# Transformer block on one core: the first two Strassen products take operands without the norm's factor, VectorE's order is written out through the first two chunks, and x is held in half tiles

## The chip, the cores and the metric

One core of one Trainium2 chip runs the kernel. The metric is the device time of one execution in microseconds (us); three executions of the kernel before took 1358.51 to 1360.71, median 1359.51.

## What is computed

The reference is one layer of a hybrid encoder, for one sequence of 1024 positions, model width 1024, all in float32. Cut to what matters here:

```python
x = x + jnp.concatenate([y_conv, y_mla], axis=-1) @ w_o[i]

hf = rmsnorm(x, norm_ffn_g[i])
a = dwconv_centred(hf @ w_up[i], ffn_conv_w[i], ffn_conv_b[i])
g, u = jnp.split(a, 2, axis=-1)
x = x + (jax.nn.silu(g) * u) @ w_down[i]

gate = jax.nn.sigmoid(rmsnorm(x, ple_norm_g[i]) @ w_ple_gate[i])
x = x + gate * (p[i] @ w_ple_proj[i])
```

`rmsnorm(x, g)` is x times g, times one factor r per position (the inverse root of the mean square). `w_up` has 2 x 2816 columns: 22 chunks of 128 columns of g and of u.

## The kernel before, in words

**Layout.** x lies with its 1024 features on partitions, in 8 blocks of 128, and the 1024 positions along the rows. A matrix product of float32 is made of three matmuls of parts: each operand is split into a high part (rounded, made by ScalarE) and a low part (what is left, made by VectorE), and high x high, high x low and low x high are summed in PSUM. `gemm` (L135) issues these. A sum of 128 x 512 fills one of the eight banks of PSUM.

**Stages around the change.** After attention, `out_mla` (L606) adds the second half of the output projection block by block (d = 0 to 7): VectorE adds the sum to x (L625), ScalarE squares it, VectorE adds the squares to `ss`, and SyncE's queue stores the block to DRAM for later (L627). Then the position factors r of the norm are made: `norm` (L217) sums `ss` over partitions by 16 little matmuls (L228), takes the inverse root on VectorE (L233 to L242), and spreads r over all partitions by 16 more little matmuls (L253) into two banks. The little matmuls are put between the matmuls of other work. That other work is `embed` (L774): the per-layer embedding's projection, eight blocks of twelve matmuls that need neither x nor the norm.

**The chunks.** Each chunk's up projection is a Strassen-Winograd product with 7 products in place of 8: the moving operands are sums and differences of the quarters of the normed x (`up_moving`, L716; b11, b21, b22, t1 to t4, each in four blocks k, shared by all chunks), the stationary ones are sums of the weights (`stationary`, L640: a11, a12, s1 to s4, a22). Quarters: x blocks 0 to 3 or 4 to 7, positions 0 to 511 or 512 to 1023. Each product is twelve matmuls of 128 x 512. `BANK` (L672) says which products add into the same bank: 1 and 2; 6, 7 and 4; 5 and 3. After each product `read` (L793) takes the bank's sum so far, and the next product into that bank has to wait for this. With both halves of g read, VectorE and ScalarE make the convolution over positions (`conv3`, L256) and ScalarE makes Silu (L815).

**Order.** TensorE's order is that of the code throughout. VectorE's is the code's inside a `manual_schedule` block (L821 to L850), outside of which a scheduler sets it by its own estimate; ScalarE's and GpSimd's are the scheduler's always. Before, the block ends when the moving operands are made, so that the reads, the convolutions and the weights of the chunks are placed by the scheduler. TensorE's order in the stage is: embeddings 0 to 5, product 1 of chunks 0 and 1, embeddings 6 and 7, and then products 5, 2, 3, 6, 7, 4, each of chunk 0 and then of chunk 1; chunk 2 and the rest follow in `run` (L694).

Of the kernel before, what the change touches and what calls it, by code (L numbers as in the profile page):

```python
# [33 lines left out]
def tile_block(ctx, tc, xT, pT, wlat, wun, wdn, wuq, wukv, vecs, cst, out):  # L34
# [180 lines left out]


    def norm(sh, sl, dim):  # L217
        n = sh.shape[1] // P
# [4 lines left out]

        def first():
            p8.append(small())
            for t in range(n):
                for i, z in enumerate((sh, sl)):
                    tiny.append(lambda t=t, i=i, z=z: mm(p8[0][:, 2 * t:2 * t + 2], z[:, t * P:t * P + P], onesr[:, 0:2], start=i == 0, stop=i == 1))  # L228

        def root():  # L230
            v, y, t = [const.tile([P, 8], F32, name=m, bufs=2)[:, 0:n] for m in ("nv", "ny", "nt")]
            yh, yl = [const.tile([P, 8], FR, name=m, bufs=2)[:, 0:n] for m in ("nyh", "nyl")]
            ts(out=v, in0=p8[0][:, 0:2 * n:2], scalar1=1.0 / dim, scalar2=EPS, op0=ALU.mult, op1=ALU.add)  # L233
            yi = y.bitcast(I32)
            ts(out=yi, in0=v.bitcast(I32), scalar1=1, scalar2=None, op0=ALU.logical_shift_right)
            ts(out=yi, in0=yi, scalar1=-1.0, scalar2=float(0x5F3759DF), op0=ALU.mult, op1=ALU.add)
            for _ in range(3):
# [2 lines left out]
                stt(out=y, in0=t, scalar=1.5, in1=y, op0=ALU.add, op1=ALU.mult)  # L240
# [1 line left out]
            vt(out=yl, in0=y, in1=f(yh), op=ALU.subtract)  # L242
# [4 lines left out]
        def second():
            for t in range(n):
                if t % 4 == 0:
                    rs.append(small()[:, 0:min(4, n - t) * P])  # L250
                c = t % 4 * P
                for i, y in enumerate(ys):
                    tiny.append(lambda p=rs[-1][:, c:c + P], y=y[:, t:t + 1], i=i: mm(p, y.to_broadcast([P, P]), identr, start=i == 0, stop=i == 1))  # L253
# [367 lines left out]
    for d in range(NC_):  # L621
        out_mla(d, [3] if d < 3 else [0, 1, 2, 3])
        if d < 7:
            for p, s in pieces(accs[d]):
                tt(out=x1[d][:, s], in0=p, in1=x1[d][:, s], op=ALU.add)  # L625
            square_acc(ss, x1[d], d == 0, nc.vector)
        nc.sync.dma_start(out=x2d[d], in_=x1[d]) if d < 7 else None  # L627
# [86 lines left out]
    def up_moving(rs, then):  # L716
# [4 lines left out]
        def scaled(c, i):
            o = x1[c][:, HALF[i]]
            stt(out=o, in0=o, scalar=vc(V_FFN + c), in1=rs[i], op0=ALU.mult, op1=ALU.mult)

        def diff(o, p, q):
            tt(out=o, in0=p, in1=q, op=sub)  # L726

        def behind(fn):
            if low[0]:
                low[0]()  # L730
            low[0] = fn

        def put(src, h, z):
            nc.scalar.copy(out=h, in_=src)
# [50 lines left out]
    def up_unit(c, later=None):  # L785
# [6 lines left out]

        def read(i, p):  # L793
            g1, g2, u1, u2 = ag[:, T1S], ag[:, T2S], au[:, T1S], au[:, T2S]
            if i == 1:
                nc.scalar.copy(out=u1, in_=p)
# [15 lines left out]
            if i in (3, 6) and len(half) == 2:  # L812
# [2 lines left out]
                act(out=t, in_=t, func=AF.Silu)  # L815
# [6 lines left out]
    sq, sh, sl = ft(), ft(FR), xt.tile([P, S], FR, name="xt")  # L822
    for p, s in pieces(accs[7]):
        tt(out=x1[7][:, s], in0=p, in1=x1[7][:, s], op=ALU.add)
        act(out=sq[:, s], in_=x1[7][:, s], func=AF.Square)
    for s in HALF:
# [3 lines left out]
    nc.sync.dma_start(out=x2d[7], in_=x1[7])  # L830
# [9 lines left out]
    for d in range(6):  # L840
        if d == 2:
            norm_first()
        if d == 4:
            norm_second()
# [1 line left out]
        if d == 2:
            norm_root()
        if d == 4:
            up_moving(rs, lambda: pair.append(up_unit(1, weights1)))
# [1 line left out]
    weights1.pop()()
    for i in (1, 5, 2, 3, 6, 7, 4):
        for unit in pair:
            unit.step(i)
        if i == 1:
            embed(6)
            embed(7)
    for c in range(2, NFF):
# [267 lines left out]
```

## Time and profile before

The profiled execution is one of the same program. Busy time is the time in which an engine has an instruction in it.

| | |
|---|---|
| median of three executions | 1359.51 us |
| the profiled execution | 1359.67 us |
| its span, first to last instruction | 1357.7 us |
| TensorE (PE) busy | 1325.2 us, 98% |
| VectorE (DVE) busy | 1006.2 us, 74% |
| ScalarE (ACT) busy | 597.0 us, 44% |
| GpSimd (POOL) busy | 256.5 us, 19% |
| mean granted clock of TensorE | 0.989 |

In the lists of instructions a row has: start and duration in us from the start of the span, engine, line of the kernel, operation, tiles out<-in, shape, count, and in brackets how long the engine had been idle before and what ended that. Names are those of the tiles: `xt` holds x, `b` the moving operands, `wm` and `whi`/`wlo` the weights, `bk` a PSUM bank, `tmp` working tiles. PEclk is the clock granted to TensorE as a share of full speed.

### The profile page before, as it was taken

To read this page: it belongs to the slowest core of one execution; us is meant where nothing else is said; L and a number is where in the kernel's file an instruction comes from. 1 tells how busy PE (TensorE), PEld (TensorE's weight loads), DVE (VectorE), ACT (ScalarE), POOL (GpSimd) and SP (SyncE) were. 2 spreads that over 40 slices of the span, in tenths; PEclk is the share of its full clock that TensorE was granted. 3 is DMA by queue.
4 is the path that set the end of the run, shared out by engine and by line. 5 is a ranking of instruction groups with operands and counts; after the bars stand their busy time and mean duration, and the time that the engine had idled before them with its cause. 6 is when DMAs were issued, how large, how long until landed. Compare 5 with 4: busy or idle time off the path is not lost.

```text
span 1357.7 us, 16448 instructions
## 1 busy us (share of the span) xinstructions
PE 1325.2 (98%) x6354; PEld 1089.3 (80%) x6354; DVE 1006.2 (74%) x1336; ACT 597.0 (44%) x839; POOL 256.5 (19%) x214
## 2 busy tenths in 40 slices
PE   9999999999999999879999999999998999999997
PEld 7877788888888887658888888888877888888897
DVE  7478923799999957988888888888665555557787
ACT  5323422688888834543443444344331111125433
POOL 0276452455545510000000000000000000000000
PEclk9999999999999999979999999999999999999998
DMA  6201134200000154203222222222165232121123
GB/s 210 83 31 47 47 125 155 78 1 17 1 17 1 64 215 171 93 16 124 78 78 78 94 78 78 78 93 74 66 233 216 96 98 94 55 78 51 52 81 113
DMA packets 38894, 117.38 MB, mean 86 GB/s; under 512 B 4256, under 2 KB 9632, under 8 KB 38816
## 3 DMA queue, kind: packets, MB, share of 16 engines
q1 hardware_dynamic: 36976, 111.49, 23.3%
q10 hardware_dynamic: 1840, 4.83, 0.9%
q8 instruction: 50, 0.82, 0.3%
q14 instruction: 28, 0.23, 0.1%
HBM read 88.00 MB, written 28.31 MB: 86 GB/s over the span
## 4 chain that ended last, share of the span: by engine, by line
PE 87%; DVE 9%; issue 2%; DMA 1%; ACT 1%; POOL 1%; POOLq 0%; SPq 0%; ACTq 0%
PE bk L139 55%; PE big L139 12%; PE small L139 4%; PE small L534 4%; PE small L547 2%; PE big L504 2%; PE big L508 2%; PE big L506 2%; PE small L546 2%; DVE tmp L163 1%; DVE xt L726 1%; DVE b L726 1%; DMA x<-x2d 1%; DVE tmp L262 1%; DVE rbc L164 0%
## 5 line engine op out<-in xcount | busy, mean ns | idle before, releaser
L139 PE MATMUL bk<-gu,whi 128*128 128x512 f32 x704 | 194.4, 397 | 4.1 <-DVE x L904 3.5
L139 PE MATMUL bk<-b,wm 128*128 128x512 f32 x792 | 192.8, 396 | 1.7 <-DVE b L726 1.4
L139 PEld LDWEIGHTS bk<-b,wm 128*128 128x128 f32 x792 | 148.5, 188 | 38.7 <-DVE b L726 2.5
L139 PEld LDWEIGHTS bk<-gu,whi 128*128 128x128 f32 x704 | 132.7, 189 | 37.1 <-issue 3.9
L904 DVE TENSOR_TENSOR x<-bk,x 128x512 f32<-128x512 f32 x112 | 72.0, 686 | 90.0 <-PE bk L139 87.3
L139 PE MATMUL bk<-xt,wm 128*128 128x512 f32 x528 | 129.4, 399 | 7.4 <-DVE xt L726 5.4
L128 ACT ACTIVATE whi<-wraw 128x1024 fp32r<-128x1024 f32 (+2 forms) x55 | 51.3, 933 | 193.0 <-PE bk L139 140.2
L139 PEld LDWEIGHTS bk<-xt,wm 128*128 128x128 f32 x528 | 100.9, 192 | 32.5 <-DVE xt L726 7.7
L139 PE MATMUL bk<-b,whi 128*128 128x512 f32 x352 | 112.3, 399 | 3.1 <-DVE b L726 3.1
L646 POOL TENSOR_TENSOR wm<-wraw,wm 128x512 fp32r<-128x512 f32 x22 | 28.8, 1309 | 449.2 <-ACT wm L645 449.2
L139 PE MATMUL bk<-gu,wlo 128*128 128x512 f32 x352 | 111.3, 397 | 0.0
L790 DVE TENSOR_TENSOR tmp<-bk,tmp 128x512 f32<-128x512 f32 x110 | 75.6, 688 | 30.7 <-PE bk L139 30.6
L521 POOL TENSOR_SCALAR tmp<-tmp,sm 128x256 f32<-128x256 f32 x64 | 70.1, 1095 | 101.4 <-DVE sm L514 98.8
L261 ACT ACTIVATE tmp<-tmp,vec 128x1024 f32<-128x1024 f32 x44 | 54.4, 1237 | 71.0 <-DVE tmp L790 71.0
L511 DVE TENSOR_REDUCE mx<-big 128x1 f32<-128x1024 f32 x64 | 78.0, 1219 | 10.3 <-PE big L508 9.8
L537 DVE TENSOR_TENSOR ptl<-small,pth 128x512 fp32r<-128x512 f32 x128 | 83.1, 680 | 1.2 <-ACT pth L536 0.9
L139 PEld LDWEIGHTS bk<-b,whi 128*128 128x128 f32 x352 | 66.9, 190 | 20.5 <-DVE b L726 4.4
L262 DVE SCALAR_TENSOR_TENSOR tmp<-tmp,vec 128x1023 f32<-128x1023 f32 x48 | 63.9, 1331 | 21.5 <-ACT tmp L261 19.0
L139 PEld LDWEIGHTS bk<-gu,wlo 128*128 128x128 f32 x352 | 66.4, 189 | 16.1
L536 ACT CAST pth<-small 128x512 fp32r<-128x512 f32 x128 | 68.9, 591 | 19.8 <-PE small L534 17.3
L971 POOL TENSOR_TENSOR tmp<-x,rf 128x256 f32<-128x256 f32 x3 | 2.1, 727 | 385.2 <-ACT rf L966 385.2
L139 PE MATMUL big<-hh,whi 128*128 128x512 f32 x224 | 71.8, 402 | 3.1 <-DVE tmp L414 3.1
(290 smaller groups left out, 2863.0 us busy)
## 6 DMA issues: line engine op xcount, KB each, us to landing
wraw<-in_wun_dram SPq DMA_DIRECT2D x73, 512.0 KB, 3.2
gud<-tmp SPq DMA_DIRECT2D x22, 512.0 KB, 2.6
tmp<-gud SPq DMA_DIRECT2D x22, 512.0 KB, 4.0
wraw<-in_wdn_dram SPq DMA_DIRECT2D x24, 384.0 KB, 3.1
tmp<-in_xT_dram SPq DMA_DIRECT2D x15, 512.0 KB, 4.2
x1d<-tmp SPq DMA_DIRECT2D x8, 512.0 KB, 2.8
xt<-x1d SPq DMA_DIRECT2D x8, 512.0 KB, 6.7
x2d<-xt SPq DMA_DIRECT2D x8, 512.0 KB, 2.7
```

Source lines behind the costliest of these rows:

```text
L128: act(out=wh, in_=raw, func=AF.Copy)
L139: mm(p, w, x[:, s], start=a, stop=z, skip_group_check=more)
L261: act(out=t, in_=src, func=AF.Identity, scale=vc(w + 1), bias=vc(bias))
L262: stt(out=t[:, 1:S], in0=src[:, 0:S - 1], scalar=vc(w), in1=t[:, 1:S], op0=ALU.mult, op1=ALU.add)
L511: nc.vector.tensor_reduce(m, p, AX.X, ALU.max, negate=True)
L521: nc.gpsimd.tensor_scalar(out=e[:, w:S], in0=e[:, w:S], scalar1=su, scalar2=None, op0=ALU.mult)
L534: nc.tensor.transpose(t[:, k, :], e[:, (g * 4 + k) * P:(g * 4 + k) * P + P], ident)
L536: nc.scalar.copy(out=pth[:, ks, qs], in_=t)
L537: tt(out=ptl[:, ks, qs], in0=t, in1=f(pth)[:, ks, qs], op=ALU.subtract)
L646: eng.tensor_tensor(out=z, in0=src, in1=f(h), op=ALU.subtract)
L790: add = lambda o, p, q: tt(out=o, in0=p, in1=q, op=ALU.add)
L904: tt(out=x1[d][:, s], in0=q, in1=x1[d][:, s], op=ALU.add)
```

## The change

It has four parts.

1. The moving operands b11 and b21 are split from x times the gain g alone (`raw_moving`), before r is known. r is put on the sums when they are read: VectorE multiplies the sums of products 1 and 1 + 2 by r in place of a copy by ScalarE. This holds for all 22 chunks. ScalarE copies r from the two banks to SBUF once (`rr`). The other moving operands are made of the normed x as before, one small function each (`put_t1`, `put_b22`, `put_t3`, `put_t2`, `put_t4`).
2. Product 1 and then product 2 of chunk 0 follow embedding 3, ahead of embeddings 4 to 7; product 1 and 2 of chunk 1 follow these; then 5, 5, 3, 3, 6, 6, 7, 7, 4, 4. The squares' little matmuls stand in embedding 1, those of r in embedding 3.
3. The block in which VectorE's order is the code's now reaches to the end of chunks 0 and 1, with the reads (`got`), both gate convolutions and chunk 2's weights in it.
4. x is held in 16 tiles of 128 x 512 instead of 8 of 128 x 1024, and loaded, added to, squared and stored by halves.

The core of the diff:

```diff
     for d in range(NC_):
-        nc.sync.dma_start(out=x1[d], in_=x1d[d])
+        for x, s in zip(x1[d], HALF):
+            nc.sync.dma_start(out=x, in_=x1d[d][:, s])
...
-        def step(self, i):
+        def step(self, i, read=True):
...
-            self.read(i, p)
+            if read:
+                self.got(i)
+
+        def got(self, i):
+            self.read(i, self.banks[BANK[i]])
...
+    def raw_moving(name, c0, tiles):
         for k in range(4):
+            x, g = x1[c0 + k][0], vc(V_FFN + c0 + k)
+            h, z = tiles(k)
+            act(out=h, in_=x, func=AF.Copy, scale=g)
+            behind(lambda x=x, g=g, h=h, z=z: stt(out=z, in0=x, scalar=g, in1=f(h), op0=ALU.mult, op1=ALU.subtract))
+            bs[k][name] = (h, z)
+        behind(None)
...
-            if i == 1:
-                nc.scalar.copy(out=u1, in_=p)
+            if i in (1, 2):
+                tt(out=u1 if i == 1 else g1, in0=p, in1=rr[:, T1S], op=ALU.mult)
             elif i == 5:
                 add(u2, p, u1)
-            elif i == 2:
-                nc.scalar.copy(out=g1, in_=p)
...
+    raw_moving("b11", 0, lambda k: (b1(), b1()))
+    embed(0)
+    embed(1, norm_first)
+    norm_root()
     for j in range(2):
         embed_weights(j)
...
+    raw_moving("b21", 4, lambda k: [z[:, T1S] for z in b2s[k]])
+    embed(2)
+    norm_second()
+    embed(3)
+    u0 = pair[0]
+    u0.step(1, False)
+    for i in range(2):
+        nc.scalar.copy(out=rr[:, HALF[i]], in_=rs[i])
+    put_t1(0, rs)
+    put_t1(1, rs)
+    u0.got(1)
+    u0.step(2, False)
...
+    for d in range(4, NC_):
         embed(d)
...
+    u0.step(6, False)
+    put_t4(1)
+    put_t4(2)
+    u0.got(6)
+    u1.step(6, False)
+    put_t4(3)
+    behind(None)
+    u1.got(6)
+    u2 = up_unit(2, weights1)
+    u0.step(7)
+    weights1.pop()()
+    u1.step(7)
+    u0.step(4)
+    u1.step(4)
     dve_order.close()
```

VectorE, ahead of `out_mla(6)` (`s14` and `s23` are sums of chunk 0's weights; `big_4753` and `big_4725` are the sum of block 4; `wlo_4834` and `wlo_4800` the low part of the weights that block 6 needs). Before:

```order
L625 TENSOR_TENSOR xt_4545<-big_4725,xt_4545 128x1024
L654 TENSOR_TENSOR s14_4873<-wraw_4867 128x512
L657 TENSOR_TENSOR s23_4874<-wraw_4865,wraw_4867 128x512
L655 TENSOR_TENSOR s23_4874<-s14_4873,wraw_4865 128x512
L280 TENSOR_TENSOR tmp_4650<-tmp_4650,tmp_4751 128x1024
L656 TENSOR_TENSOR s14_4873<-wraw_4865,s23_4874 128x512
L625 TENSOR_TENSOR xt_4546<-big_4761,xt_4546 128x1024
L129 TENSOR_TENSOR wlo_4800<-wraw_4797,whi_4799 128x1024
```

The same place after:

```order
L664 TENSOR_TENSOR s14_4916<-wraw_4910 128x512
L667 TENSOR_TENSOR s23_4917<-wraw_4908,wraw_4910 128x512
L633 TENSOR_TENSOR xt_4554<-big_4753,xt_4554 128x512
L633 TENSOR_TENSOR xt_4550<-big_4753,xt_4550 128x512
L665 TENSOR_TENSOR s23_4917<-s14_4916,wraw_4908 128x512
L666 TENSOR_TENSOR s14_4916<-wraw_4908,s23_4917 128x512
L637 TENSOR_TENSOR tmp_4667<-tmp_4667,tmp_4778 128x1024
L656 TENSOR_TENSOR wm2_4923<-s14_4916,wm2_4922 128x1024
L633 TENSOR_TENSOR xt_4555<-big_4792,xt_4555 128x512
L633 TENSOR_TENSOR xt_4551<-big_4792,xt_4551 128x512
L129 TENSOR_TENSOR wlo_4834<-wraw_4831,whi_4833 128x1024
```

The first two sums moved ahead of block 4's add, and the low part of s14 (`wm2_4923`) ahead of `wlo_4834`.

VectorE, around the reads of product 6 (L790 before, L807 after; `bk_5380` and `bk_5417` are chunk 0's bank for 6, 7 and 4, `bk_5399` and `bk_5448` chunk 1's; L262 and L263, after L264 and L265, are the convolution). Before:

```order
L726 TENSOR_TENSOR xt_5202<-xt_4548,xt_5201 128x512 x2
L790 TENSOR_TENSOR tmp_4891<-bk_5380,tmp_4891 128x512
L262 SCALAR_TENSOR_TENSOR tmp_5394<-tmp_4891,vec_71,tmp_5394 128x1023
L263 SCALAR_TENSOR_TENSOR tmp_5394<-tmp_4891,vec_71,tmp_5394 128x1023
L790 TENSOR_TENSOR tmp_5107<-bk_5399,tmp_5107 128x512
L790 TENSOR_TENSOR tmp_4892<-bk_5380,tmp_4892 128x512
```

After:

```order
L807 TENSOR_TENSOR tmp_4934<-bk_5417,tmp_4934 128x512
L264 SCALAR_TENSOR_TENSOR tmp_5443<-tmp_4934,vec_71,tmp_5443 128x1023
L265 SCALAR_TENSOR_TENSOR tmp_5443<-tmp_4934,vec_71,tmp_5443 128x1023
L754 SCALAR_TENSOR_TENSOR xt_4557<-xt_4557,vec_71,rr_4539 128x512
L750 TENSOR_TENSOR xt_4557<-xt_4557,xt_4553 128x512
L750 TENSOR_TENSOR xt_5439<-xt_4556,xt_5438 128x512
L750 TENSOR_TENSOR xt_5464<-xt_4557,xt_5463 128x512
L807 TENSOR_TENSOR tmp_5269<-bk_5448,tmp_5269 128x512
```

The making of the last moving operand, t4 of block 3 (`xt_5464` is its low part), moved between chunk 0's convolution and chunk 1's read of product 6. On ScalarE the cast `xt_5463` that it needs now stands behind the table load and Silu of chunk 0.

VectorE, ahead of the read of chunk 0's product 7. Before, that read is the last row of the first fence on product 6 (`tmp_4892<-bk_5380`), and chunk 1's gate convolution comes behind it. After:

```order
L264 SCALAR_TENSOR_TENSOR tmp_5469<-tmp_5269,vec_71,tmp_5469 128x1023
L265 SCALAR_TENSOR_TENSOR tmp_5469<-tmp_5269,vec_71,tmp_5469 128x1023
L656 TENSOR_TENSOR wlo_5479<-wraw_5474,whi_5478 128x1024
L664 TENSOR_TENSOR s14_5482<-wraw_5476 128x512
L656 TENSOR_TENSOR wlo_5658<-wraw_5653,whi_5657 128x1024
L665 TENSOR_TENSOR s23_5483<-s14_5482,wraw_5474 128x512
L666 TENSOR_TENSOR s14_5482<-wraw_5474,s23_5483 128x512
L667 TENSOR_TENSOR s23_5483<-wraw_5474,wraw_5476 128x512
L656 TENSOR_TENSOR wm2_5489<-s14_5482,wm2_5488 128x1024
L807 TENSOR_TENSOR tmp_4935<-bk_5417,tmp_4935 128x512
```

The split of chunk 2's weights (and one row of chunk 3's, `wlo_5658`) moved ahead of the read.

More of the change, by code (lines that the diff above doesn't have):

```diff
@@ L623, in tile_block @@
         if d < 7:
[L624 to L627, printed above, removed]
+            q = ss if d == 0 else ft()
+            for p, x, s in zip(accs[d] if isinstance(accs[d], list) else halves(accs[d]), x1[d], HALF):
+                tt(out=x, in0=p, in1=x, op=ALU.add)
+                act(out=q[:, s], in_=x, func=AF.Square)
+                nc.sync.dma_start(out=x2d[d][:, s], in_=x)
+            if d:
+                tt(out=ss, in0=ss, in1=q, op=ALU.add)
         if d in (3, 4):
@@ new lines, in tile_block, with behind @@
+    identr = b1()[:, 0:P]
+    nc.scalar.copy(out=identr, in_=ident)
+    wjt = [(b1(), b1()) for _ in range(2)]
+    low = [None]
+    bs = [{} for _ in range(4)]
+    def behind(fn):
+        if low[0]:
+            low[0]()
+        low[0] = fn
+    def raw_moving(name, c0, tiles):
+        for k in range(4):
+            x, g = x1[c0 + k][0], vc(V_FFN + c0 + k)
[3 more added lines that the diff above has]
+            bs[k][name] = (h, z)
+        behind(None)
@@ new lines, in diff, with scaled, put, put_t1 @@
+    def diff(o, p, q):
+        tt(out=o, in0=p, in1=q, op=ALU.subtract)
+    def scaled(c, i, r=None):
+        o = x1[c][i]
+        stt(out=o, in0=o, scalar=vc(V_FFN + c), in1=rr[:, HALF[i]] if r is None else r, op0=ALU.mult, op1=ALU.mult)
+    def put(src, h, z):
+        nc.scalar.copy(out=h, in_=src)
+        behind(lambda: diff(z, src, f(h)))
+        return h, z
+    y1, y2 = x1[0:4], x1[4:8]
+    def put_t1(k, rs=(None, None)):
+        for i in range(2):
+            scaled(k, i, rs[i])
+        diff(y1[k][0], y1[k][1], y1[k][0])
+        bs[k]["t1"] = put(y1[k][0], b1(), b1())
@@ L774, in embed @@
-    def embed(d):
+        wj.append(load_unit(wun[U_PROJ + 1][:, j * 512:j * 512 + 512], 512, wjt[j]))
+    def embed(d, between=None):
         acc = [bank(), bank()]
@@ L779, in embed @@
             gemm(acc, w[0][:, c], w[1][:, c], ph[k][0], ph[k][1], k == 0, k == 1)
+            if k == 0 and between:
+                between()
         t = ft()
@@ L821, in tile_block @@
     dve_order.enter_context(tc.manual_schedule(engines={mybir.EngineType.DVE}))
[L822 to L826, printed above, removed]
+    sq, sh = ft(), halves(ft(FR))
+    for p, x, s in zip(accs[7], x1[7], HALF):
+        tt(out=x, in0=p, in1=x, op=ALU.add)
+        act(out=sq[:, s], in_=x, func=AF.Square)
+        nc.sync.dma_start(out=x2d[7][:, s], in_=x)
+    for h, z, s in zip(sh, sl, HALF):
         tt(out=ss[:, s], in0=ss[:, s], in1=sq[:, s], op=ALU.add)
-        nc.vector.tensor_copy(out=sh[:, s], in_=ss[:, s])
-        tt(out=sl[:, s], in0=ss[:, s], in1=f(sh)[:, s], op=ALU.subtract)
-    nc.sync.dma_start(out=x2d[7], in_=x1[7])
+        nc.vector.tensor_copy(out=h, in_=ss[:, s])
+        tt(out=z, in0=ss[:, s], in1=f(h), op=ALU.subtract)
     ps_done()
@@ L837, in tile_block @@
     norm_first, norm_root, norm_second, rs = norm(sh, sl, D)
+    b2s = [(b2(), b2()) for _ in range(4)]
+    raw_moving("b11", 0, lambda k: (b1(), b1()))
+    embed(0)
+    embed(1, norm_first)
+    norm_root()
     for j in range(2):
         embed_weights(j)
[L840 to L844, printed above, removed]
-        embed(d)
[L846 to L849, printed above, removed]
-    dve_order.close()
[L851 to L858, printed above, removed]
+    raw_moving("b21", 4, lambda k: [z[:, T1S] for z in b2s[k]])
[4 more added lines that the diff above has]
+    u0.step(1, False)
+    for i in range(2):
+        nc.scalar.copy(out=rr[:, HALF[i]], in_=rs[i])
[3 more added lines that the diff above has]
+    u0.step(2, False)
+    put_t1(2)
+    put_t1(3)
+    behind(None)
+    u0.got(2)
+    for d in range(4, NC_):
+        embed(d)
+    u1 = up_unit(1, weights1)
+    u1.step(1, False)
+    put_b22(0)
+    put_b22(1)
+    u1.got(1)
+    u1.step(2, False)
+    put_b22(2)
+    put_b22(3)
+    behind(None)
+    u1.got(2)
+    u0.step(5, False)
+    put_t3(0)
+    put_t3(1)
+    put_t3(2)
+    put_t3(3)
+    u0.got(5)
+    u1.step(5, False)
+    put_t2(0)
+    put_t2(1)
+    u1.got(5)
+    u0.step(3, False)
+    put_t2(2)
+    put_t2(3)
+    behind(None)
+    u0.got(3)
+    weights1.pop()()
+    u1.step(3, False)
+    put_t4(0)
+    u1.got(3)
+    u0.step(6, False)
[4 more added lines that the diff above has]
+    put_t4(3)
+    behind(None)
+    u1.got(6)
+    u2 = up_unit(2, weights1)
+    u0.step(7)
+    weights1.pop()()
+    u1.step(7)
+    u0.step(4)
+    u1.step(4)
+    dve_order.close()
+    run(u2)
+    for c in range(3, NFF):
         run(up_unit(c))
```

82 lines of the change are left out of this document (25 added, 57 removed).

## The prediction

> **What bounds the kernel now.** I read the page's busy shares first, then the busy times cut by stage, then who waited for whom in the changed stage, then the instructions in order of time. Columns of the stages: length, then busy us of TensorE, weight loads, VectorE, ScalarE, GpSimd, then the granted clock.
>
> ```profile
> 475.70:524.30 48.60, 47.24 (x211) 37.89 (x210) 29.61 (x29) 16.44 (x20) 3.56 (x5) 1.00 0.49 181
> 524.30:545.80 21.50, 20.59 (x106) 16.99 (x106) 15.72 (x34) 12.32 (x22) 1.29 (x1) 1.00 0.59 214
> 545.80:581.70 35.90, 31.06 (x121) 23.08 (x120) 33.89 (x47) 19.20 (x28) 0.00 (x0) 0.95 0.20 77
> 581.70:611.20 29.50, 22.06 (x74) 15.37 (x73) 25.14 (x35) 13.11 (x15) 1.30 (x1) 0.77 0.06 18
> 611.20:1000.00 388.80, 388.80 (x1679) 315.06 (x1678) 311.50 (x333) 158.42 (x179) 24.91 (x19) 1.00 0.24 88
> ```
>
> From 611.2 on TensorE is never idle; in the changed stage, 524.3 to 611.2, it is idle 13.2 us and partly at a low clock, while VectorE is busy 33.9 of 35.9 us in the middle. So VectorE's queue sets the pace there. TensorE's waits in that stage (total, count, longest) end mostly on VectorE:
>
> ```profile
> PE bk L139 <- DVE xt L726: 5.4, 4, 2.9
> PE bk L139 <- DVE b L726: 4.5, 4, 2.1
> PE bk L139 <- ACT xt L734: 1.8, 1, 1.8
> ...
> PE bk L139 <- DVE tmp L790: 0.3, 1, 0.3
> ```
>
> In order of time, the lines on which the sum stands (the wait before each in brackets):
>
> ```profile
> 525.67 0.97 PE L139 MATMUL bk<-tmp,whi 128*128 128x512 f32 x3 [0.91 <-DVE xt L824]
> ...
> 545.78 0.63 PE L139 MATMUL bk<-b,whi 128*128 128x512 f32 x2
> ...
> 567.43 0.49 PE L139 MATMUL bk<-b,whi 128*128 128x512 f32 x1 [1.04 <-DVE b L726]
> ...
> 570.48 0.59 PE L139 MATMUL bk<-b,whi 128*128 128x512 f32 x1 [2.09 <-DVE b L726]
> ...
> 576.13 5.76 PE L139 MATMUL bk<-b,wm 128*128 128x512 f32 x24
> 581.73 0.40 PE L139 MATMUL bk<-xt,wm 128*128 128x512 f32 x1
> 585.00 1.65 PE L139 MATMUL bk<-xt,wm 128*128 128x512 f32 x3 [2.88 <-DVE xt L726]
> ...
> 594.57 5.10 PE L139 MATMUL bk<-xt,wm 128*128 128x512 f32 x14 [0.96 <-DVE xt L726]
> ...
> 611.16 0.63 PE L139 MATMUL bk<-b,whi 128*128 128x512 f32 x2
> ```
>
> Twenty-four matmuls take 581.73 - 576.13 = 5.60 us, so 0.233 us each and 2.80 for a product of one chunk (twelve) or an embedding. 611.16 is chunk 2's first matmul. The change is judged by when that comes, because all after it is the same TensorE work without a gap. I write "0p1" for chunk 0's product 1 and "read" for the VectorE instruction that takes its sum.
>
> **Ahead of the stage: 0.7 us later.** The change also lets the scheduler put two sums of chunk 0's weights (L664, L667) ahead of the residual add of block 4. Before:
>
> ```profile
> 506.12 0.62 ACT L645 CAST wm<-wraw 128x512 fp32r<-128x512 f32 x1 [3.47 <-DMA wraw<-in_wun_dram]
> ...
> 511.97 1.04 ACT L645 CAST wm<-s 128x1024 fp32r<-128x1024 f32 x1
> ```
> ```profile
> 505.87 1.23 DVE L625 TENSOR_TENSOR xt<-big,xt 128x1024 f32<-128x1024 f32 x1 [1.96 <-PE big L139]
> ...
> 512.72 1.21 DVE L129 TENSOR_TENSOR wlo<-wraw,whi 128x1024 fp32r<-128x1024 f32 x1
> 513.86 1.22 DVE L646 TENSOR_TENSOR wm<-s,wm 128x1024 fp32r<-128x1024 f32 x1
> ```
>
> The weights land at 506.1. Now the add waits behind them and 1.2 us of sums, and the low part of one of the sums (L646 above, L656 after the change; 513.86 - 512.72 = 1.14 from issue to issue) stands ahead of the low part L129 for which TensorE waits. Counted down: sums 506.2 to 507.4, adds to 508.6, two dependent sums to 510.0, square sum to 511.1, L656, which needs ScalarE's cast, to 512.3, two adds to 513.4, L129 ends 514.6 instead of 513.9. Bounds: 0 (the scheduler's earlier order was as tight) to 1.8, if GpSimd's weight instruction holds VectorE up (below). I take 0.7; the stage's clock starts at 525.0.
>
> **To the end of 0p1: earlier by 3.6 us.** In before 525.67 to 545.78 holds six embeddings, 71 matmuls (16.6 us), and 3.5 us of the 32 little matmuls of the norm. Now four embeddings and 0p1: 59 matmuls, 13.8 us, and the same 3.5. The norm's root is needed sooner. Its rows:
>
> ```profile
> 534.75 0.17 DVE L233 TENSOR_SCALAR nv<-bk 128x8 f32<-128x8 f32 x1 [3.16 <-PE bk L228]
> ...
> 535.76 1.23 DVE L240 SCALAR_TENSOR_TENSOR ny<-nt,ny 128x8 f32<-128x8 f32 x1
> ...
> 538.44 0.17 DVE L242 TENSOR_TENSOR nyl<-ny,nyh 128x8 fp32r<-128x8 f32 x1
> 540.39 1.41 DVE L723 SCALAR_TENSOR_TENSOR xt<-xt,vec,bk 128x512 f32<-128x512 f32 x2 [1.78 <-PE bk L253]
> ```
> ```profile
> 535.68 1.29 POOL L646 TENSOR_TENSOR wm<-wraw,wm 128x512 fp32r<-128x512 f32 x1 [27.51 <-ACT wm L645]
> ```
>
> One L240 took 1.23 instead of 0.17 us while GpSimd's a22 ran; without it the chain is 2.8 us. Now ScalarE does four scalings ahead of the last two squares, which makes the norm's sums about 1.7 later, and VectorE has four low parts (0.6 each) ahead of the root; so the chain ends at 537.7, TensorE waits 0.9 us for it, and 0p1 ends at 545.0, not 548.6. GpSimd's a22 moves to about 540, among the low parts: 0 to 1.1 us, taken as 0, since VectorE's instruction and GpSimd's can also pass each other.
>
> **The new waits.** 0p2 adds into the bank of 0p1, so TensorE, with the four embeddings queued behind it, waits for VectorE's read of 0p1. A 512-wide instruction costs VectorE 0.60, by the first row below ((2.49 - 0.69) / 3), one that takes the norm from PSUM 0.66 by the L723 row.
>
> ```profile
> 587.88 2.49 DVE L726 TENSOR_TENSOR xt<-xt 128x512 fp32r<-128x512 f32 x4
> ...
> 597.82 1.28 DVE L262 SCALAR_TENSOR_TENSOR tmp<-tmp,vec 128x1023 f32<-128x1023 f32 x1 [1.31 <-ACT tmp L261]
> 599.14 1.28 DVE L263 SCALAR_TENSOR_TENSOR tmp<-tmp,vec 128x1023 f32<-128x1023 f32 x1
> 600.34 0.68 DVE L790 TENSOR_TENSOR tmp<-bk,tmp 128x512 f32<-128x512 f32 x1
> ```
>
> Between root and read stand two weight low parts (1.2, and 0.3 for ScalarE), four low parts (2.4), four scalings (2.7), two differences that wait for them (1.4), a low part (0.6); the read takes 0.7. So 537.7 + 9.3 = 547.0: a wait of 2.1. 0p2 and embeddings 4 to 7 run to 561.1, 1p1 to 563.9. The read of 1p1 comes right after, 0.8 with both hand-overs; 1p2, 0p5, 1p5 run to 573.2. Then 0p3 needs the read of 0p5, behind which VectorE has eight differences and three low parts (11 x 0.60 and 0.4 of dependence) after the read of 1p2 at 568.5: read done 576.2, a wait of 3.0. 0p3, 1p3, 0p6, 1p6 end at 587.4; the read of 0p6 comes at 587.9, wait 0.5; 0p7 ends at 590.7.
>
> Now 1p7 needs the read of 1p6. The fixed order puts chunk 0's gate convolution and the last low part, t4(3), ahead of that read, and ScalarE's queue puts its table load and Silu ahead of the cast that this low part needs:
>
> ```profile
> 596.55 1.24 ACT L261 ACTIVATE tmp<-tmp,vec 128x1024 f32<-128x1024 f32 x1 [2.59 <-DVE tmp L790]
> 600.50 1.28 ACT L815 ACT_TABLE_LOAD   x1 [2.71 <-DVE tmp L263]
> 601.80 1.06 ACT L815 ACTIVATE tmp<-tmp 128x1024 f32<-128x1024 f32 x1
> ```
> ```profile
> 593.34 0.62 ACT L734 CAST xt<-xt 128x512 fp32r<-128x512 f32 x1 [0.59 <-DVE xt L726]
> ```
>
> 587.9 + 1.24 + 1.28 + 1.28 + 1.28 + 1.06 + 0.62 + 0.68 + 0.68 = 596.0: a wait of 5.3. In before nothing that TensorE needed lay behind that chain. 1p7 ends at 598.8. Then 0p4 needs the read of 0p7, and ahead of it stand chunk 1's convolution (1.24 + 1.28 + 1.28, from 596.0 to 599.8) and the split of chunk 2's weights: three 1024-wide (3 x 1.14), four 512-wide (4 x 0.60), 0.6 for ScalarE, the read 0.7: 606.9, a wait of 8.1. 0p4 and 1p4 end at 612.6. So at full clock chunk 2 starts at 612.6 instead of 611.2: **+1.4 us**. The old waits are gone (13.2 us, and what the low clock cost behind them), and new ones of 0.9 + 0.9 + 2.1 + 0.8 + 3.0 + 0.5 + 5.3 + 8.1 = 21.6 us take their place.
>
> **The clock.** After waits the profile grants half speed:
>
> ```profile
> 570.80:573.80 3.00, 3.00 (x8) 2.13 (x7) 2.93 (x5) 1.35 (x2) 0.00 (x0) 0.50 0.00 0
> ...
> 585.00:598.00 13.00, 8.74 (x17) 5.21 (x18) 10.98 (x18) 5.39 (x7) 0.00 (x0) 0.50 0.12 40
> ```
>
> At half speed 14 matmuls took 5.10 us from 594.57, less 0.17 for the last's end 4.9 against 3.3: 1.6 lost. Before 0p4 TensorE has run 2.8 of 16 us, so it starts slow: 1.6 by that row, 2.8 if all twelve are slow; I take 2.2, on the path, as TensorE is not idle again. (The slow 1p7 is hidden by the 8.1.) The waits of 2.1 and 3.0 are like the 1.04 and 2.09 with three matmuls between that brought the 0.50 of 570.8: each may cost 0 or 1.6; I take one. Together 2.2 + 1.6 = **3.8 us**. Beside this the Trainium skill, "TensorE: Matmul & The Clock Gate", Part 1, says that half rate follows an idle window of about 3.4 us. The trace goes lower: 2.09 us were enough there, with 1.04 shortly ahead. By the page alone the two middle waits would cost nothing.
>
> **What costs nothing.** x in halves gives SyncE 16 more issues of this kind, 0.3 us each and 5 us in all, in a queue that otherwise stands idle from its last store to the next weights:
>
> ```profile
> 525.64 0.32 SPq L830 DMA_DIRECT2D x2d<-xt  x1
> ```
>
> None of them is ahead of a load that is late, so 0, with a bound of 0.3. The two copies of the norm's rows (0.6 each) go to ScalarE, which is busy 19.2 of 35.9 us. In all 22 chunks the read of product 1 and that of 2 move from ScalarE to VectorE; in the steady stage one of the two kinds is
>
> ```profile
> L796 ACT COPY tmp<-bk 128x512 f32<-128x512 f32 x19 | 10.9, 574 | 0.8 <-PE bk L139 0.8
> ```
>
> VectorE is busy 311.5 of 388.8 us there; 1.2 more in each chunk's 19.6 (seven products) raises 80% to 86%. TensorE's next matmul into those banks is two products later, so this is 0 until VectorE falls a product behind.
>
> **Sum.** +1.4 + 3.8 = +5.2 us. The span 1357.7 becomes 1362.9; the profiled execution's 1359.67 (2.0 more than its span) becomes 1364.9; against the median, 1359.51, **1364.7**. A measurement of this kernel can tell about 0.2%, 2.7 us, from no change: faster is under 1356.8, slower over 1362.2.
>
> **Rivals, with chances.** The forecast has 0.42.
> Only the two long waits lower the clock (what the page's rule would give): 1.4 + 2.2 = +3.6, 1363.1. For it: each of the middle waits stands between long dense runs; against it, the 0.50 after 2.09. 0.25.
> Full clock at 0p4 too, or as much found elsewhere: +1.4, 1360.9, no change. Against it stands every row with the 0.50. 0.13.
> Both middle waits lower the clock, and GpSimd's a22 holds VectorE 1.1: 5.2 + 1.6 + 1.1 = +7.9, 1367.4. 0.08.
> The steady stage pays: 0.7, one read, for each of 20 chunks: 5.2 + 14 = +19.2, 1378.7. Against: no idle time there now. 0.05.
> The other side: VectorE isn't late at the end. If it reaches the reads of 1p6 and 0p7 before TensorE is done with 0p7 and 1p7 (by 590.7 and 598.8, 5.3 and 8.1 us sooner than I count), both waits and the slow 0p4 go: 5.2 - 5.3 - 8.1 - 2.2 = -10.4, 1349.1. For it: the old order reached those reads with a wait of 0.3. Against: the rows ahead of the reads are fixed and all have prices. 0.07.
> The range, 1360.0 to 1368.6, holds the first four with 0.9 and 1.2 to spare for VectorE's and the first stage's bounds. Slower: 0.42 + 0.25 + 0.08 + 0.05 = 0.80; within 0.2%: 0.13; faster: 0.07.
>
> **What would show it.** In the new profile: 0p1's matmuls start at about 542, and embeddings 4 to 7 after 0p2; TensorE's longest waits end on the reads: 5 us before 1p7 and 5 to 8 before 0p4 (less where 1p7 ran slow), at 0.50 clock behind; chunk 2 starts 4 to 6 us later; the time from there to the end is unchanged. Wrong, if no wait over 3 us stands before 1p7 and 0p4, or if TensorE is idle after chunk 2's start.

## The result and the profile after

The changed kernel took 1367.80 to 1370.54 us in six executions, median 1369.45; the kernel before, beside it, 1358.21 to 1361.81, median 1359.90. The ratio is 1.0069, interval 1.0056 to 1.0082: slower by 9.5 us, where 5.2 were forecast. The direction is right; the median lies 0.9 us beyond the upper end of the range. The profiled execution took 1367.80 us with a span of 1366.0, 8.3 more than the span before.

The stages of the changed kernel, cut at embedding 0, the end of product 1 of chunk 0 (0p1), the start of 0p3 and the start of chunk 2 (columns as in the prediction: length, busy us of TensorE, weight loads, VectorE, ScalarE, GpSimd, then the granted clock, the DMA engines' busy share and GB/s):

```profile
523.20:543.90 20.70, 18.28 (x93) 14.52 (x91) 17.41 (x37) 15.10 (x27) 1.30 (x1) 1.00 0.48 179
543.90:578.70 34.80, 25.73 (x108) 20.14 (x109) 28.41 (x44) 16.90 (x27) 0.00 (x0) 1.00 0.30 106
578.70:619.50 40.80, 28.39 (x96) 21.89 (x97) 33.13 (x43) 14.02 (x15) 1.30 (x1) 0.79 0.07 26
619.50:1000.00 380.50, 380.50 (x1643) 308.37 (x1642) 330.19 (x367) 135.23 (x133) 39.69 (x19) 1.00 0.23 83
```

From chunk 2 on TensorE is still never idle, with VectorE up from 303 to 330 of the 380.5 us. From there to the last instruction it is 746.5 us in both kernels, as the prediction said, so the whole loss lies ahead of 619.5. Chunk 2 starts 8.3 us later than before (611.16), where 4 to 6 were forecast. Who waited for whom ahead of it (total, count, longest):

```profile
PE bk L139 <- DVE tmp L807: 15.4, 4, 6.8
PE bk L139 <- DVE tmp L813: 6.3, 2, 3.3
PE bk L255 <- DVE nyh L243: 0.9, 1, 0.9
PE bk L139 <- DVE xt L839: 0.9, 1, 0.9
```

The waits for operands (`xt`, `b` by L726 in the kernel before) are gone. Those for reads (`tmp`: L813 takes products 1 and 2, L807 the others) stand in their place. In order of time on TensorE:

```profile
523.20 0.40 PE L139 MATMUL bk<-tmp,whi 128*128 128x512 f32 x1
...
546.67 0.73 PE L139 MATMUL bk<-b,whi 128*128 128x512 f32 x2 [2.99 <-DVE tmp L813]
...
549.57 11.36 PE L139 MATMUL bk<-tmp,b 128*128 128x512 f32 x48
...
566.99 0.73 PE L139 MATMUL bk<-b,whi 128*128 128x512 f32 x2 [3.26 <-DVE tmp L813]
...
578.71 7.38 PE L139 MATMUL bk<-b,wm 128*128 128x512 f32 x24 [3.05 <-DVE tmp L807]
585.92 5.61 PE L139 MATMUL bk<-xt,wm 128*128 128x512 f32 x24
592.02 3.07 PE L139 MATMUL bk<-b,wm 128*128 128x512 f32 x12 [0.49 <-DVE tmp L807]
600.20 4.39 PE L139 MATMUL bk<-b,wm 128*128 128x512 f32 x12 [5.11 <-DVE tmp L807]
611.40 8.26 PE L139 MATMUL bk<-xt,wm 128*128 128x512 f32 x24 [6.81 <-DVE tmp L807]
619.50 0.63 PE L139 MATMUL bk<-b,whi 128*128 128x512 f32 x2
```

The bracketed rows are 0p2, 1p2, 0p3, 0p7, 1p7 and 0p4, each of which adds to a bank that VectorE has to read first. Twenty-four matmuls take 5.61 us at full clock, but 7.38 and 8.26 behind two of the waits. The one wait that the forecast had much smaller is that ahead of 1p2. Its cause stands on VectorE and in the chain of waits:

```profile
560.19 0.69 DVE L750 TENSOR_TENSOR b<-xt,b 128x512 fp32r<-128x512 f32 x1
566.25 0.69 DVE L813 TENSOR_TENSOR tmp<-bk,rr 128x512 f32<-128x512 f32 x1 [5.37 <-DMA pjd<-tmp]
```
```profile
559.04 7.08 DMA pjd<-tmp
```

The read of 1p1 writes into a `tmp` tile from which embedding 6 was still being stored. The sum was there by 563.7, but VectorE stood until 566.2 for the store, which took 7.08 us. In the 35 us around it (issues, size of each, median us to landing):

```profile
pjd<-tmp ACTq DMA_DIRECT2D x5, 512.0 KB, 2.9
wraw<-in_wun_dram SPq DMA_DIRECT2D x2, 512.0 KB, 6.3
```

The stores of embeddings 3, 4 and 5 took 2.6, 2.6 and 2.9 us, those of 6 and 7 took 7.08 and 5.5. The two weight loads, issued from 557.17 on, were under way beside the last two; what a store takes beside loads alone was not tried.

### The profile page after: what moved, and what is told of

Same layout as the page of the kernel before. It is cut to its first block, busy times and chain, and to the rows that moved or that the text cites. A ratio compares the mean times of both kernels' runs of the same rounds, so it can differ in the third digit from the quotient of the medians.

```text
span 1366.0 us, 16434 instructions
## 1 busy us (share of the span) xinstructions
PE 1322.0 (97%) x6354; PEld 1089.0 (80%) x6354; DVE 1032.7 (76%) x1390; ACT 579.3 (42%) x808; POOL 271.6 (20%) x214
## 4 chain that ended last, share of the span: by engine, by line
PE 82%; DVE 10%; issue 2%; DMA 2%; POOL 2%; ACT 2%; POOLq 0%; SPq 0%; ACTq 0%; DVEq 0%
PE bk L139 54%; PE big L139 8%; PE small L139 4%; PE small L536 4%; PE small L549 2%; PE big L506 2%; PE big L510 2%; PE big L508 2%; PE small L548 2%; DVE tmp L163 1%; DVE xt L750 1%; DVE tmp L265 1%; DVE tmp L264 1%; DMA x<-x2d 1%; DMA pjd<-tmp 1%
## 5 line engine op out<-in xcount | busy, mean ns | idle before, releaser
L139 PE MATMUL bk<-xt,wm 128*128 128x512 f32 x528 | 126.6, 396 | 6.8 <-DVE tmp L807 6.8
L656 POOL TENSOR_TENSOR wm<-wraw,wm 128x512 fp32r<-128x512 f32 x22 | 44.0, 1999 | 444.7 <-ACT wm L655 444.7
L807 DVE TENSOR_TENSOR tmp<-bk,tmp 128x512 f32<-128x512 f32 x110 | 75.4, 687 | 29.7 <-PE bk L139 29.7
L263 ACT ACTIVATE tmp<-tmp,vec 128x1024 f32<-128x1024 f32 x44 | 54.5, 1238 | 74.4 <-DVE tmp L807 74.3
L515 ACT ACTIVATE tmp<-big,mx 128x1024 f32<-128x1024 f32 x64 | 72.1, 1127 | 5.2 <-DVE sm L516 2.6
```

The lines of the kernel that those rows point to most:

```text
L139: mm(p, w, x[:, s], start=a, stop=z, skip_group_check=more)
L263: act(out=t, in_=src, func=AF.Identity, scale=vc(w + 1), bias=vc(bias))
L515: act(out=e, in_=p, func=AF.Exp, bias=m, accum_out=su)
L656: eng.tensor_tensor(out=z, in0=src, in1=f(h), op=ALU.subtract)
L807: add = lambda o, p, q: tt(out=o, in0=p, in1=q, op=ALU.add)
```

## The experiments

Runs are compared through the ratio to the kernel before, on the same chip. Inside the trace I use one distance: from embedding 0's first matmul to the first matmul of chunk 2's product 6 (in the changed kernel 523.20 and 622.30, so 99.10 us; in the kernel before 524.36 and 613.96, so 89.60). The difference, 9.50 us, is the change's price in the stage.

| kernel | distance, us | median, us | ratio to before, interval |
|---|---|---|---|
| before | 89.60 | 1359.90 | 1 |
| changed | 99.10 | 1369.45 | 1.0069, 1.0056 to 1.0082 |
| embedding 6 in half tiles | 96.46 | 1367.20 | 1.0061, 1.0048 to 1.0073 |
| chunk 2's weights later | 92.55 | 1362.10 | 1.0025, 1.0014 to 1.0036 |
| convolutions later | 91.94 | 1361.47 | 1.0020, 1.0010 to 1.0029 |
| one wait filled | 98.29 | 1367.90 | 1.0064, 1.0052 to 1.0077 |
| scheduler's order | 89.94 | 1360.97 | 1.0013, 1.0004 to 1.0021 |
| first three together | 84.47 | 1353.96 | 0.9968, 0.9955 to 0.9980 |
| new order | 81.98 | 1350.61 | 0.9948, 0.9934 to 0.9962 |
| five waits filled | 93.31 | 1364.50 | 1.0045, 1.0033 to 1.0058 |
| changed, again | 99.25 | 1371.06 | 1.0083, 1.0069 to 1.0096 |
| half tiles, again | 98.35 | 1367.88 | 1.0063, 1.0049 to 1.0077 |
| new order, second | 76.84 | 1352.97 | 0.9955, 0.9942 to 0.9967 |

**The store.** Embedding 6 leaves from two tiles of the pool of x:

```diff
+        if d == 6:
+            for p, s in pieces(acc):
+                t = bt(F32)
+                nc.scalar.copy(out=t, in_=p)
+                nc.scalar.dma_start(out=pjd[d][:, s], in_=t)
+            return
         t = ft()
```

> The changed kernel with one edit: embedding 6 leaves through two half tiles that the norm no longer needs, not through a tile that chunk 1's up sums reuse. In the changed kernel VectorE stands 5.4 us for that store ahead of its read of 1p1, and TensorE waits 3.26 us behind 1p1 where 0.8 was forecast. Theory (a wait that the order did not show, 2.4 us on the path): the DMA wait goes, the wait behind 1p1 falls to about 0.9 us, all that follows comes 2.4 us earlier, 1367.0 us, ratio 1.0052 to the kernel before. Rival (VectorE's queue is late behind it whatever the store does): the wait reappears ahead of 0p3 or 0p6, gain under 0.5 us, ratio 1.0066 or more.

VectorE's read of 1p1 and TensorE's 1p2 in that kernel (with its edit L819 reads products 1 and 2, and L813 the others):

```profile
565.44 0.69 DVE L819 TENSOR_TENSOR tmp<-bk,rr 128x512 f32<-128x512 f32 x1 [2.89 <-PE bk L139]
```
```profile
566.18 0.73 PE L139 MATMUL bk<-b,whi 128*128 128x512 f32 x2 [0.78 <-DVE tmp L819]
```

Now the read waits for TensorE alone, and 1p2 for 0.78 us, the forecast's 0.8. The two half stores still took 7.2 us each (median), but nothing waits for them. The distance is 2.64 shorter. The ratio, 1.0061, did not tell the theories apart, so both kernels were run once more on one chip.

> The changed kernel itself, on the chip of the next two, so that the store's share is compared on one chip. Both theories: ratio about 1.007, 9 to 10 us over the kernel before, and product 6 of chunk 2 begins 99 us behind embedding 0's first matmul, as in its first trace (99.10).

> The kernel with embedding 6 in half tiles once more, since its first comparison (1.0061, interval 1.0048 to 1.0073) lay between both theories. Theory (the store's wait costs 2.4 us of the end): median 1.8 to 2.8 us under that of the changed kernel on this chip, product 6 of chunk 2 at 96.5 us behind embedding 0. Rival (slow stretches or later waits give it back): median less than 1 us under it.

The changed kernel's distance came back, 99.25; its median is 12.4 us over the kernel before, where 9 to 10 were expected. The medians are 1371.06 and 1367.88, 3.2 us apart, a little more than the theory's 1.8 to 2.8; the two intervals still overlap a little. The second distance, 98.35, missed its 96.5, because here 0p2 ran at half clock: it took 4.45 us (546.82 to 551.27), not 2.90. I take 2.5 us for the store, the difference of the two waits ahead of 1p2 (3.26 and 0.78).

**Chunk 2's weights.**

```diff
-    u2 = up_unit(2, weights1)
     u0.step(7)
-    weights1.pop()()
     u1.step(7)
+    u2 = up_unit(2, weights1)
+    weights1.pop()()
     u0.step(4)
```

> The changed kernel with chunk 2's weight sums put behind VectorE's reads of 0p7 and 1p7, not ahead of them. Theory (the fixed order puts a block of 6.6 us, 604.06 to 610.65, ahead of the read that 0p4 needs): the wait of 6.8 us ahead of 0p4 falls under 1 us, 0p4 and 1p4 take 5.8 us and not 8.3, chunk 2 starts 7 to 9 us earlier, 1360.5 to 1362.5 us, ratio 1.0005 to 1.002. Rival (the block is needed by chunk 2's first products, so the wait only moves behind chunk 2's start): chunk 2's products wait 3 us or more, gain under 4 us, ratio 1.004 or more.

In the changed kernel this stands ahead of the read of 0p7 (at 610.57):

```profile
603.98 1.22 DVE L656 TENSOR_TENSOR wlo<-wraw,whi 128x1024 fp32r<-128x1024 f32 x1
...
609.43 1.23 DVE L656 TENSOR_TENSOR wm<-s,wm 128x1024 fp32r<-128x1024 f32 x1 [0.56 <-ACT wm L655]
610.57 0.69 DVE L807 TENSOR_TENSOR tmp<-bk,tmp 128x512 f32<-128x512 f32 x1
```

With the block behind the read, TensorE goes from 1p7 to 0p4 without a wait and at full speed; the weights are 0.29 us late for chunk 2's product 6:

```profile
603.12 4.47 PE L139 MATMUL bk<-b,wm 128*128 128x512 f32 x12 [5.12 <-DVE tmp L807]
607.72 5.74 PE L139 MATMUL bk<-xt,wm 128*128 128x512 f32 x24
...
616.10 0.63 PE L139 MATMUL bk<-xt,wm 128*128 128x512 f32 x2
617.02 2.60 PE L139 MATMUL bk<-xt,wm 128*128 128x512 f32 x10 [0.29 <-DVE wm L656]
```

The theory's mechanism holds, though the ratio, 1.0025, is a little over its range: 0p2 and 1p2 ran at half clock in this trace. The distance fell by 6.6 us, of which product 6 gives back 0.6: it takes 3.36 us to the next product's start (619.46), and 2.74 in the kernel before.

**The convolutions.** `read` puts chunk 0's and chunk 1's gate convolution and Silu into a list, which is worked off behind `u1.step(7)`.

```diff
-                tpool[0] = tmpb
-                t = conv3(ag, V_FW + 6 * c, V_FB + 2 * c)
-                act(out=t, in_=t, func=AF.Silu)
-                out_.append(t)
+                def gate():
...
+                gates.append(gate) if c < 2 else gate()
...
     u1.step(7)
+    gates.pop(0)()
+    gates.pop(0)()
     u0.step(4)
```

> The changed kernel with the gate convolutions and Silus of chunks 0 and 1 put behind VectorE's reads of 0p7 and 1p7; chunk 2's weight sums stay where they are. Theory (the chain sum of 0p6, convolution, table load and Silu, half tile of t4, read of 1p6 makes the 5.1 us ahead of 1p7): that wait falls under 1 us, 1p7 takes 2.9 us and not 4.4; the read of 0p7 still stands behind the block of 6.6 us, so 3 to 4 us are left ahead of 0p4; chunk 2 starts 7 to 10 us earlier, 1359.5 to 1362.5 us, ratio 0.9997 to 1.002. Rival (VectorE has just so much to do up to there, so the wait moves to 0p4 and to chunk 2): gain under 3 us, ratio 1.0047 or more.

```profile
599.78 3.07 PE L139 MATMUL bk<-b,wm 128*128 128x512 f32 x12 [0.35 <-DVE tmp L807]
607.06 7.33 PE L139 MATMUL bk<-xt,wm 128*128 128x512 f32 x24 [4.21 <-DVE tmp L807]
```

1p7 now waits 0.35 us and runs at full clock, and 4.2 are left ahead of 0p4, close to the theory's 3 to 4; the ratio, 1.0020, is at the end of its range. In the changed kernel one sees ScalarE's part of that chain, the table load and Silu ahead of the cast for t4(3):

```profile
595.96 1.28 ACT L830 ACT_TABLE_LOAD   x1 [2.72 <-DVE tmp L265]
597.26 1.06 ACT L830 ACTIVATE tmp<-tmp 128x1024 f32<-128x1024 f32 x1
598.22 0.60 ACT L757 CAST xt<-xt 128x512 fp32r<-128x512 f32 x1
```

**The clock.** The next kernels fill waits with matmuls into a spare bank.

```diff
     u1.step(7)
+    wbk = bank()
+    for i in range(26):
+        mm(wbk, u0.a["a11"][0][:, 0:P], bs[0]["b11"][0], start=True, stop=True)
     u0.step(4)
```

> The changed kernel with 26 matmuls of 512 columns, whose sums nobody reads, between 1p7 and 0p4, 6.1 us at 0.235 us each, where TensorE waits 6.8 us. Theory (the wait itself lowers the clock of what comes next): the read of 0p7 comes as before, but 0p4 and 1p4 take 5.8 us and not 8.3, chunk 2 starts 2.5 us earlier, 1367.0 us, ratio 1.0052. Rival (0p4 and 1p4 are slow for another reason, such as operands that come late): they still take about 8 us, 1369.5 us or more, ratio 1.0069 or more.

```profile
608.65 6.33 PE L921 MATMUL bk<-b,whi 128*128 128x512 f32 x26
614.82 5.61 PE L139 MATMUL bk<-xt,wm 128*128 128x512 f32 x24
```

0p4 and 1p4 take 5.61 us instead of 8.26. So their slowness comes from the idle time ahead and not from their operands: 2.65 us. The median does not show it: 1.0064 lies between the theory's 1.0052 and the rival's 1.0069. In this trace 0p4 began 1.8 us later, counted from embedding 0, than in the changed kernel's, mainly because 1p2 ran at half clock. Hence all five waits:

> The changed kernel with matmuls of 512 columns, whose sums nobody reads, in its five waits: 11 ahead of 0p2, 12 ahead of 1p2, 11 ahead of 0p3, 19 ahead of 1p7 and 26 ahead of 0p4, each a little less than the wait at 0.235 us each. VectorE's reads come as before. Theory (the waits lower the clock, and the slow stretches of 1.6 us at 0p3, 1.5 at 1p7 and 2.5 at 0p4 are their price): all these products run at full speed, 4 to 6 us less, 1363.5 to 1365.5 us, ratio 1.0025 to 1.004. Rival (the slow stretches are hidden, since the next read is late anyway): only the 2.5 us of 0p4 goes, ratio 1.005 or more.

Of the waits for L807's reads 2.7 us are left, and no product is slow (0p3 and 1p3 5.84 us, 1p7 3.07, 0p4 and 1p4 5.71). The distance fell by 5.8, the ratio to 1.0045. Of the 5.8, 1.6 are 0p3's and 2.5 are 0p4's; 0.6 lie ahead of 1p2, and 1.1 come from one instruction (the low part of a weight of chunk 3) that here stands behind the read of 0p7 and not ahead of it. The ratio is just over the theory's range, and its interval, 1.0033 to 1.0058, reaches into the rival's; it is the trace that decides.

**Fixed order or operands?** VectorE's block ends behind embedding 3:

```diff
     norm_second()
     embed(3)
+    dve_order.close()
...
-    dve_order.close()
     run(u2)
```

> The changed kernel, but VectorE's fixed order ends behind embedding 3, and the scheduler orders what follows, as it did there in the kernel before. Theory (the price lies in the places that the fixed order gives to the reads): the scheduler puts the read of 0p1 behind some ten more sums of operands, so a wait of 8 to 9 us stands ahead of 0p2 and another of about 7 ahead of 1p2, both followed by a slow stretch of 2.5 us; the waits of 3.05, 5.1 and 6.8 us ahead of 0p3, 1p7 and 0p4 go. About 17 us of waits where the changed kernel has 22.6, 1364 to 1367 us, ratio 1.003 to 1.005. Rival (operands without the norm cost the time, whatever the order): ratio 1.0065 or more. Second rival (only the fixed order costs): ratio 1.000 or less.

```profile
555.06 1.22 PE L139 MATMUL bk<-b,whi 128*128 128x512 f32 x2 [10.03 <-DVE tmp L813]
...
579.12 1.22 PE L139 MATMUL bk<-b,whi 128*128 128x512 f32 x2 [4.94 <-DVE tmp L813]
584.00 11.36 PE L139 MATMUL bk<-b,wm 128*128 128x512 f32 x48
```

The scheduler makes two waits where it was expected to, and none behind them. The gain was larger than I had written, 1.0013 where 1.003 to 1.005 stood: I had counted 17 us of waits and got 15, and had not credited the slow stretches that went. That is nearer to the second rival (1.000 or less) than to my range. The first rival is out: the operands without the norm, TensorE's order and the half tiles are all still in this kernel, and its distance is 89.94, the kernel before's 89.60. So nearly the whole 9.5 us go with VectorE's order alone; in the scheduler's order the rest of the change brings nothing either. What each part of that rest costs or brings was not taken apart.

**All three edits, and a new order.**

> The changed kernel with the three edits together: embedding 6 leaves from half tiles, chunk 2's weight sums come behind the read of 0p7, the two gate convolutions behind the read of 1p7. Theory: the waits behind 1p1, ahead of 1p7 and ahead of 0p4 fall from 3.3, 5.1 and 6.8 to 0.8, under 1 and 2 to 3 us, with 3 to 4 us of slow matmuls; 13 us less up to chunk 2, of which the moved convolutions give back 1 to 2: 1357 to 1360 us, ratio 0.998 to 1.000. Rival (VectorE has no room, the work only arrives later): chunk 2's or chunk 3's products wait instead, ratio 1.002 or more, no better than one edit alone.

It came out at 0.9968, better than its range (0.998 to 1.000): 4.5 us under the kernel before. The last step keeps products of one bank apart:

```diff
     u0.got(1)
+    embed(4)
     u0.step(2, False)
...
     u1.got(1)
-    u1.step(2, False)
...
     u0.step(5, False)
     put_t3(0)
+    u1.step(2, False)
```

and moves the reads of 0p2 and 1p2 to the end, 0p3 and the read of 0p5 forward.

> The last kernel, with TensorE's and VectorE's order changed as well so that two products of one bank never follow each other: embedding 4 between 0p1 and 0p2, 0p5 between 1p1 and 1p2, 0p3 behind 1p5 with its read moved ahead; the reads of 0p2 and 1p2, which nothing waits for, go to the end. Theory (same-bank products back to back make the rest of the waits): the waits of 3.0 us behind 0p1 and 3.05 us ahead of 0p3 go, with the slow stretch of 1.6 us, and some 3 us come back ahead of 0p4; 1353 to 1357 us, ratio 0.995 to 0.998. Rival (VectorE's work up to chunk 2 is the bound, not its order): ratio as of the kernel with three edits, within 0.001.

```profile
546.70 0.73 PE L139 MATMUL bk<-b,whi 128*128 128x512 f32 x2 [0.29 <-DVE tmp L819]
...
565.77 0.73 PE L139 MATMUL bk<-b,whi 128*128 128x512 f32 x2 [2.00 <-DVE tmp L819]
...
578.61 5.63 PE L139 MATMUL bk<-xt,wm 128*128 128x512 f32 x24
585.38 3.07 PE L139 MATMUL bk<-b,wm 128*128 128x512 f32 x12 [1.15 <-DVE tmp L813]
...
598.14 4.35 PE L139 MATMUL bk<-xt,wm 128*128 128x512 f32 x12 [3.55 <-DVE tmp L813]
```

1350.61 us, ratio 0.9948: with the same operands and half tiles, 7.8 us under the kernel before. That is just beyond the theory's range (0.995 to 0.998) and beyond the rival's (0.9968, within 0.001), though the intervals of the two kernels overlap a little. The waits behind 0p1 and ahead of 0p3 went; new ones stand ahead of 1p2 and 1p4. Is more to be had by order?

> The kernel of the new order with three reads moved forward once more: the read of 1p1 between the half tiles b22 of 1 and 2, the read of 0p5 ahead of the third t3, the read of 1p7 right behind chunk 2's first weight difference. Theory A (the waits of 2.0 us ahead of 1p2 and 3.55 us ahead of 1p4 are an order's fault): both go, 3 to 4 us less, 1346.5 to 1348 us, ratio 0.992 to 0.993. Theory B (VectorE works without a break from 559 to 593 us there, so an earlier read makes another operand late): the waits move to 1p3, 0p6 and chunk 2's product 6, ratio within 0.001 of 0.9948.

The waits ahead of 1p2 and 1p4 went, but 2.5 us came up ahead of 1p3, and in chunk 2 there are now (L821 and L815 are the same two reads in this kernel)

```profile
607.57 0.74 PE L139 MATMUL bk<-b,whi 128*128 128x512 f32 x2 [1.88 <-DVE tmp L821]
...
613.11 7.29 PE L139 MATMUL bk<-b,wm 128*128 128x512 f32 x24 [2.47 <-DVE tmp L815]
```

so that the kernel is no faster, 0.9955: theory B, whose range that is. Product 6 of chunk 2 comes earlier than in any other kernel, at 76.84, and the time is lost behind it. In the kernel of the new order VectorE is busy 35.0 of the 35.6 us ahead of chunk 2's weights:

```profile
558.50:594.10 35.60, 32.10 (x130) 25.05 (x129) 35.00 (x52) 12.61 (x21) 0.00 (x0) 0.95 0.13 48
```

There the amount of its work is probably the bound, no longer the order; a kernel with less work for VectorE was not run.

## Why the prediction was too small

**By its own steps.** The prediction's places, counted from embedding 0's first matmul (its clock put that at 525.0; its 1.6 us of clock for a middle wait are counted from 1p7 on), against the trace:

| start of | forecast | measured | late by |
|---|---|---|---|
| 0p2 | 22.1 | 23.47 | 1.4 |
| 1p2 | 39.7 | 43.79 | 4.1 |
| 0p3 | 51.2 | 55.51 | 4.3 |
| 1p7 | 72.6 | 77.00 | 4.4 |
| 0p4 | 83.5 | 88.20 | 4.7 |
| chunk 2 | 91.4 | 96.30 | 4.9 |

Two steps failed, both waits for VectorE ahead of a second product of one bank; from 0p3 on the sum holds to within 0.6 us.

- **"The read of 1p1 comes right after, 0.8 with both hand-overs."** It stood behind a store, 2.7 us of the 4.9, of which the experiment took back 2.5. Embeddings and chunks shared this pool before the change too, but the change put the read of 1p1 on TensorE's path, one product behind embedding 7. The prediction looked at what stood ahead of the read in VectorE's queue and not at what the tile it writes had last been used for.
- **The wait of 2.1 for the read of 0p1** was 2.99, which is 0.9 of the 4.9; and 0p1 ended 0.5 later than counted. The copies of r were costed at nothing, "ScalarE, which is busy 19.2 of 35.9 us"; but the second stood behind a cast that waited for chunk 1's weights, and VectorE waited for that copy:

```profile
541.90 0.75 DVE L754 SCALAR_TENSOR_TENSOR xt<-xt,vec,bk 128x512 f32<-128x512 f32 x1 [0.84 <-ACT rr L867]
```

  This is read from the trace; no run took it away.

**What was right.** The two long waits were forecast as 5.3 and 8.1 us and are 5.11 and 6.81 (1p7 ran slow, as was said); experiments that take away the convolutions or the weights take away the one or the other. The wait of 3.0 ahead of 0p3 is 3.05. The clock was put at 3.8 us, 2.2 + 1.6, and is 4.1, 2.5 + 1.6; filling the waits removes it. The steady stage pays nothing. GpSimd's instruction at 541.46 held nothing up. The rival in which VectorE is not late at the end came about only by another order: in the kernel with three edits the waits ahead of 1p7 and of the products 4 are 0.36 and 1.99 us. The rival nearest to the result, 1367.4, is not what this trace shows: only one of the two middle waits was followed by a slow stretch.

**Ahead of the stage** 0.7 us were forecast; embedding 0 starts 1.2 earlier than before. But in the twelve traces with this code up to there it starts between 523.10 and 525.09, and before's 524.36 lies among them: nothing is shown either way. With this the spans add up: chunk 2 is 4.9 later than forecast from embedding 0, embedding 0 is 1.9 earlier than forecast, and the span grew by 8.3, 3.1 more than 5.2. That the profiled execution, 1367.80, lies within the range is owed to that early start, and so to luck.

**The clock's rule.** The prediction set the trace's 2.09 us against the Trainium skill, "TensorE: Matmul & The Clock Gate", Part 1. The wait ahead of 0p2 settles more. It was 2.99, 3.06, 3.05 and 3.27 us in four traces where 0p2 then took 2.9 us, and 3.19, 3.12, 2.80 and 3.26 in four where it took 4.45; two kernels were profiled twice, and the one with half tiles stands in both groups. Ahead of 0p3 stood 2.97 to 3.05 us in eight traces, and seven of them had the slow stretch. Ahead of 1p2, waits of 3.26 and 3.48 us in the two traces of the changed kernel left it at 2.9 us, but 3.34 (one wait filled) was followed by 5.3 us, and 2.58 (weights later), 2.55 (convolutions later) and 2.00 (new order) by 4.4. So the length alone does not decide. The same part of the Trainium skill's page also says that the windows over which the clock is set run freely, whenever the kernel starts. That fits these waits, which do not sort by length; the windows themselves no run here shows. For a wait of 2 to 3.5 us a share of 1.6 us is to be counted and not a yes or no: half of these waits or more were followed by the slow stretch.

**What stays open.** The median lost 9.5 and on the second chip 12.4 us, the traces 8.3 in span. Both profiled executions of the changed kernel were the shortest of theirs. That the others also ran 0p2 slowly is a possible reason: on the second chip the three longer ones have a mean granted clock of 0.986 and 0.987, the profiled one 0.990. Where they ran slowly was not shown.

## What to carry to other kernels

When an order is written out by hand, ask of each instruction not only what stands ahead of it in its queue but who last used the tile that it writes: a store that is mostly over in 3 us took 7 here, with two loads under way beside it. Put the reads for which another engine waits ahead of work that is needed later, and keep products of one bank apart: the same change with three moves went from 0.7% slower to 0.3% faster, and with a new order to 0.5%. Moving reads forward stopped helping where VectorE had hardly any idle time left.
